# Output projection begun between the score groups of the last head pair

## The chip, the cores and the metric

The kernel runs on one core of one Trainium2 chip. The metric is device time in microseconds of one execution. The runs shown of the kernel before lie between 1240.41 and 1241.53 us, with a median of 1241.26 us.

## The reference

Two layers, each a hybrid mixer and a gated feed-forward block, with a layer norm behind each. x is 512 tokens by 1024, all in float32.

```python
proj = x @ w_in
qa = apply_rope(split_heads(qa, 8), cos_a, sin_a)      # 8 heads of 64, ka alike
ya = merge_heads(head_norm(dilated_attention(qa, ka, va)))
yr = merge_heads(head_norm(retention(qr, kr, vr))) * silu(gr)
yg = merge_heads(head_norm(og)) * silu(rg)             # og: gated linear attention
y = concatenate([ya, yr, yg], -1) * mix_scale          # 512 + 256 + 256 columns
mix = y @ w_out
x = layer_norm(ALPHA * x + mix, ln1_g, ln1_b)
ffn = (silu(gate) * val) @ w_down                      # gate, val = conv(x @ w_up)
x = layer_norm(ALPHA * x + ffn, ln2_g, ln2_b)
```

The dilated attention's three branches are one softmax over all earlier tokens, with a mask and a multiplicity per distance.

## The kernel before, in words

**Products.** Tokens are cut into 4 tiles of 128, and each product of matrices is three matmuls (`mm3`, L212 to L216): both sides are split into a rounded high part and a low part, and high by high, high by low and low by high are summed in PSUM. A weight tile of 128 x 1024 numbers is loaded by SyncE into one of two `raw` buffers; ScalarE (ACT) casts it to the high part `whi` (L198), and VectorE (DVE) subtracts this to get the low part `wlo` (L199), in five buffers each. So a cast waits until the last matmul that reads a buffer has ended, and a load until the subtraction that reads its `raw` buffer has. `made` lists the last matmul of every `mm3`.

**The attention.** The 8 heads of `ya` are handled in 4 pairs. For a pair, `scores` (L626 to L668) makes the scores of the 4 query tiles in three groups: tile 3, tile 2, and tiles 0 and 1 together, for both heads. Each group takes a PSUM bank per head, of four `sm` banks. A group is full matmuls (128 rows) and then matmuls on 64 rows for the low parts. VectorE reads a bank with a mask and takes the maximum (L660), ScalarE takes the exponential (L663), VectorE multiplies by the multiplicity and sums (L664). `weighted` (L669 to L704) transposes the probabilities (L288), ScalarE copies them out (L693), and they are multiplied with the values (L681), in the groups of key tiles (2, 3), (1,) and (0,); then the result is copied (L700) and transposed back. `finish` normalizes it, and `finish_rows` (L711) transposes it to rows `yt[p2]` for the output projection; it is called between the next pair's `scores` and `weighted`, and for pair 3 within `out0`.

**The mixer's end.** While the scores are made, the projections of the other parts run: `v` and the heads of pairs 2 and 3 beside pairs 0 and 1, `gates` beside pair 2. After pair 3's code, four blocks of the gated retention and linear attention, `ynat`, are transposed in the one `side` bank and scaled to rows by `to_rows` (L350 on ScalarE, L351 on VectorE), as `yt[4]` to `yt[7]`. Then `token_gemm` (L394) multiplies the rows with `w_out`, in two halves of 512 columns, `out0` and `out1`: four PSUM banks, one for each token tile, over 8 blocks of rows; for the last `tail` blocks it goes token tile by token tile. `out0` has a tail of 4, `out1` one of 8. `residual` (L390) adds the result to x.

**The order.** A scheduler sets each engine's order when the program is built. Among the instructions it takes for ready it picks that with the lowest priority number, which `at` sets and which counts up with each instruction; what is ready it estimates itself. On the chip each engine runs its order as it stands, and waits on semaphores where data or a buffer is not there. `tc.issue_after(ins)` puts an instruction behind another one of the same engine in that order, without a semaphore. The third score group of pairs 0, 1 and 2 stands behind the 4th, 11th and 4th product of `v`, `heads` and `gates`; that of pair 3 behind nothing.

## Time and profile before

| | before |
|---|---|
| profiled execution | 1243.3 us |
| its span, first to last instruction | 1241.5 us |
| mean granted TensorE clock | 0.995 |
| TensorE matmul busy | 1224.1 us |
| VectorE busy | 794.6 us |
| ScalarE busy | 509.8 us |
| median of three runs | 1241.26 us |

PE is TensorE's matmuls, PEld its weight loads, DVE VectorE, ACT ScalarE, SP SyncE. In an order of time a row has the start in us from the span's start, the duration, engine, source line, operation and tiles; "x3" are merged instructions, and in brackets stands the idle time before, with what ended it. Matmuls overlap, so the distance of their starts tells what one costs, not its duration. In a row of stretches stand the start and end, the length, the busy time of each engine with its number of instructions, and then the granted clock, the DMA share and the GB/s. In a row of waits stand the total, the number and the longest.

### The profile page before, as it was taken

The numbers are of one execution on the slowest core, as the hardware profiler recorded it, in microseconds if no ns is written. First come the engines' busy times: TensorE is split into PE (matmuls) and PEld (weight loads), VectorE is DVE, ScalarE is ACT, GpSimd is POOL, SyncE is SP. The second block draws the span as 40 slices with busy tenths as digits, with TensorE's granted clock in tenths as the row PEclk, the third lists the DMA queues.
The fourth block names the chain that finished last, engine by engine and source line by source line (L and its number), as shares of the span: only waits on it lengthen the run. The fifth ranks groups of instructions, "written<-read, shape, count | busy, mean of one in ns | idle before, by whom it ended". The sixth has DMA issues, their size and how long they took to land.

```text
span 1241.5 us, 15145 instructions
## 1 busy us (share of the span) xinstructions
PE 1224.1 (99%) x5892; PEld 996.8 (80%) x5892; DVE 794.6 (64%) x1467; ACT 509.8 (41%) x721; POOL 17.1 (1%) x26
## 2 busy tenths in 40 slices
PE   9999999999999999999999999999999999999997
PEld 7877777898888888888887777778988888888885
DVE  6697776777663356664767867768766633566636
ACT  4435775144442134442143557652444421444410
POOL 0000000000000000000000000000000000000000
PEclk9999999999999999999999999999999999999998
DMA  8421223223332232322142122231343323333321
GB/s 289 133 66 34 86 86 102 68 85 119 102 91 88 93 115 89 88 99 77 62 128 93 35 58 79 68 119 51 103 120 91 95 77 100 112 102 102 94 77 68
DMA packets 33398, 116.26 MB, mean 94 GB/s; under 512 B 3728, under 2 KB 4144, under 8 KB 33200
## 3 DMA queue, kind: packets, MB, share of 16 engines
q1 hardware_dynamic: 32176, 111.11, 28.5%
q0 software_dynamic: 1152, 4.19, 1.1%
q8 instruction: 46, 0.75, 0.3%
q14 instruction: 24, 0.20, 0.0%
HBM read 113.20 MB, written 2.10 MB: 93 GB/s over the span
## 4 chain that ended last, share of the span: by engine, by line
PE 94%; DVE 3%; ACT 1%; DMA 1%; issue 1%; SPq 0%; DVEq 0%; ACTq 0%
PE acc L214 26%; PE acc L215 26%; PE acc L216 26%; PE bk L288 3%; PE side L214 2%; PE side L216 2%; PE side L215 2%; PE bk L681 2%; PE bk L639 1%; DMA raw<-in_wpk 1%; PE bk L567 1%; PE bk L547 1%; PE bk L563 1%; DVE wlo L199 1%; PE bk L553 1%
## 5 line engine op out<-in xcount | busy, mean ns | idle before, releaser
L199 DVE TENSOR_TENSOR wlo<-raw,whi 128x1024 fp32r<-128x1024 f32 (+2 forms) x201 | 239.9, 1195 | 231.2 <-ACT whi L198 230.5
L215 PE MATMUL acc<-xtl,whi 128*128 128x512 f32 (+1 forms) x896 | 341.9, 382 | 0.0
L214 PE MATMUL acc<-xth,whi 128*128 128x512 f32 (+1 forms) x896 | 340.8, 381 | 0.0
L216 PE MATMUL acc<-xth,wlo 128*128 128x512 f32 (+1 forms) x896 | 340.1, 380 | 0.0
L198 ACT CAST whi<-raw 128x1024 fp32r<-128x1024 f32 (+2 forms) x201 | 205.8, 1026 | 315.8 <-PE side L216 130.7
L216 PEld LDWEIGHTS acc<-xth,wlo 128*128 128x128 f32 x896 | 168.6, 188 | 35.8 <-issue 5.5
L215 PEld LDWEIGHTS acc<-xtl,whi 128*128 128x128 f32 x896 | 168.6, 188 | 33.5 <-issue 3.0
L214 PEld LDWEIGHTS acc<-xth,whi 128*128 128x128 f32 x896 | 168.3, 188 | 32.7 <-issue 2.0
L214 PE MATMUL acc<-whi,xth 128*128 128x512 f32 (+1 forms) x256 | 95.0, 371 | 0.8 <-ACT whi L198 0.8
L215 PE MATMUL acc<-wlo,xth 128*128 128x512 f32 (+1 forms) x256 | 94.9, 371 | 0.8 <-DVE wlo L199 0.7
L216 PE MATMUL acc<-whi,xtl 128*128 128x512 f32 (+1 forms) x256 | 94.1, 368 | 0.0
L214 PE MATMUL acc<-whi,yt 128*128 128x512 f32 x238 | 93.2, 393 | 0.0
L216 PE MATMUL acc<-whi,yt 128*128 128x512 f32 x238 | 92.4, 389 | 0.0
L215 PE MATMUL acc<-wlo,yt 128*128 128x512 f32 x238 | 92.3, 389 | 0.0
L796 DVE SCALAR_TENSOR_TENSOR pg<-acc,prm,pg 128x511 f32<-128x511 f32 x86 | 64.2, 747 | 31.4 <-ACT pg L795 31.4
L795 ACT ACTIVATE pg<-acc,prm 128x512 f32<-128x512 f32 x86 | 66.8, 777 | 26.0 <-PE acc L216 26.0
L797 DVE SCALAR_TENSOR_TENSOR pg<-acc,prm,pg 128x510 f32<-128x510 f32 x86 | 64.4, 749 | 3.0
L390 DVE SCALAR_TENSOR_TENSOR x<-x,acc 128x512 f32<-128x512 f32 x38 | 26.1, 686 | 59.7 <-PE acc L216 59.7
L214 PEld LDWEIGHTS acc<-whi,xth 128*128 128x128 f32 x256 | 48.1, 188 | 9.6 <-issue 1.2
L214 PE MATMUL acc<-whi,yrg 128*128 128x512 f32 x138 | 55.5, 402 | 0.0
L215 PEld LDWEIGHTS acc<-wlo,xth 128*128 128x128 f32 x256 | 48.5, 189 | 8.2 <-DVE wlo L199 1.5
L215 PE MATMUL acc<-wlo,yrg 128*128 128x512 f32 x138 | 54.9, 397 | 0.0
(182 smaller groups left out, 1538.4 us busy)
## 6 DMA issues: line engine op xcount, KB each, us to landing
raw<-in_wpk SPq DMA_DIRECT2D x188, 512.0 KB, 3.6
gb<-in_lnv POOLq DMA_DIRECT2D x8, 512.0 KB, 4.7
x<-in_x SPq DMA_DIRECT2D x4, 512.0 KB, 6.6
raw<-in_wpk SPq DMA_DIRECT2D x8, 256.0 KB, 2.8
out<-x SPq DMA_DIRECT2D x8, 256.0 KB, 2.0
raw<-in_wpk SPq DMA_DIRECT2D x4, 408.0 KB, 3.8
xraw<-in_xt SPq DMA_DIRECT2D x3, 512.0 KB, 7.6
cst<-in_cst SPq DMA_DIRECT2D x1, 1478.0 KB, 9.1
```

Source lines behind the costliest of these rows:

```text
L198: nc.scalar.copy(hi, raw)
L199: lo_engine.tensor_sub(lo, raw, hi.bitcast(F32))
L214: nc.tensor.matmul(ps, ah, bh, start=first, stop=False)
L215: nc.tensor.matmul(ps, ah, bl, start=False, stop=False)
L216: made.append(nc.tensor.matmul(ps, al, bh, start=False, stop=last).ins)
L288: nc.tensor.transpose(dst, src, ident)
L390: V.scalar_tensor_tensor(out=xr, in0=xr, scalar=scale, in1=ps, op0=ALU.mult, op1=ALU.add)
L547: mmul(sc, kT[:, ts], qbd, start=True, stop=True)
L681: mmul(oT[hh * 64:hh * 64 + 64, j * P:], vv[:, j, c0 + hh * 64:c0 + hh * 64 + 64], pts[hh][:, o:o + n], start=j == 2, stop=j == 0, skip_gr ...
L795: A.activation(out=u, in_=ps, func=AF.Identity, scale=w(2), bias=w(3))
L796: V.scalar_tensor_tensor(out=u[:, 1:], in0=ps[:, :S - 1], scalar=w(1), in1=u[:, 1:], op0=ALU.mult, op1=ALU.add)
L797: V.scalar_tensor_tensor(out=u[:, 2:], in0=ps[:, :S - 2], scalar=w(0), in1=u[:, 2:], op0=ALU.mult, op1=ALU.add)
```

## The change

The output projection's first half is made in two parts. Before pair 3's scores the gated blocks are transposed (`turn_gated`) and `out0` is begun: `token_gemm` is now a generator, which stops at the blocks in `pause`. It emits two blocks ahead of the pair's code and the rest behind it. The blocks are taken in the order pair 0, pair 1, gated, pair 2, pair 3, where the gated ones came first, and the weight tiles are packed in that order; `out0` has a tail of 3. The third score group of pair 3 stands behind the 6th product of `out0`. The probabilities' first four batches of transposes of pairs 0 and 2 stand behind the 12th, 14th, 16th and 18th product of `v` and `gates`.

```diff
-        w[f"out{h}"] = [(ks, c) for ks in (PAIRS[2], PAIRS[3], PAIRS[0], PAIRS[1])]
+        w[f"out{h}"] = [(ks, c) for ks in (PAIRS[0], PAIRS[2], PAIRS[3], PAIRS[1])]
...
-    def token_gemm(rows, kt, tail, done, between=None):
+    def token_gemm(rows, kt, tail, done, between=None, pause=()):
...
         for i in range(n - tail):
+            if i in pause:
+                yield
             for t in range(NT):
                 step(i, t)
...
             done(ps[t], t)
+        yield
...
-        def weighted(pr, c0):
+        def weighted(pr, c0, behind):
...
-                    for j in js:
-                        for i in range(j, NT):
-                            transpose(bk[:, o:o + P], pr[hh][i][:, j * P:(j + 1) * P])
-                            o += P
+                    with tc.issue_after(behind.pop(0)) if behind else nullcontext():
+                        for j in js:
+                            for i in range(j, NT):
+                                transpose(bk[:, o:o + P], pr[hh][i][:, j * P:(j + 1) * P])
+                                o += P
...
+        def turn_gated():
+
+            for k in range(4):
+                bk = side()
+                for t in range(NT):
+                    transpose(bk[:, t * P:(t + 1) * P], ynat[t][:, k * P:(k + 1) * P])
+                yt[4 + k] = to_rows(bk, mix(4 + k), "yt" if k == 3 else "yrg")
+
+        order = (0, 1, 4, 5, 6, 7, 2, 3)
...
+        def out_half(h, tail, between=None, pause=()):
...
+            return token_gemm(lambda i: yt[order[i]], kt, tail, done, between, pause)
...
+                p2 = 2 * two + u
+                if p2 == 3:
+                    at(base + 9300)
+                    turn_gated()
+                    at(base + 20000)
+                    marks["out"] = len(made)
+                    out0 = out_half(0, 3, finish_rows, (2,))
+                    next(out0)
                 at(base + 6000 + 3000 * two + 400 * u)
-                p2 = 2 * two + u
...
-                name, n = (("v", 3), ("heads", 10), ("gates", 3), (None, 0))[p2]
-                pr = scores(parts[p2], l3, made[marks[name] + n] if name else None)
+                name, n, m = (("v", 3, 11), ("heads", 10, None), ("gates", 3, 11), ("out", 5, None))[p2]
+                after = lambda n: made[marks[name] + n]
+                pr = scores(parts[p2], l3, after(n))
                 finish_rows()
-                o = weighted(pr, p2 * P)
+                o = weighted(pr, p2 * P, [after(m + 2 * i) for i in range(4)] if m else [])
...
-        order = (4, 5, 6, 7, 0, 1, 2, 3)
...
-            token_gemm(lambda i: yt[order[i]], kt, 8 if h else 4, done, None if h else finish_rows)
+        next(out0)
+        at(base + 25000)
+        next(out_half(1, 8))
```

TensorE, where the first pair's transposes begin, before; `acc` is the product of the second token tile with the values' weights, `pg` the probabilities, `cst` the identity:

```order
L214 MATMUL acc_974<-whi_924,xth_80 128x512
L215 MATMUL acc_974<-wlo_925,xth_80 128x512
L216 MATMUL acc_974<-whi_924,xtl_81 128x512
L288 MATMUL bk_1297<-cst,pg_1250 128x128
L288 MATMUL bk_1297<-cst,pg_1246 128x128 x2
L214 MATMUL acc_974<-whi_930,xth_80 128x512
L215 MATMUL acc_974<-wlo_931,xth_80 128x512
L288 MATMUL bk_1303<-cst,pg_1251 128x128
```

The same place of TensorE's order now:

```order
L214 MATMUL acc_978<-whi_934,xth_80 128x512
L215 MATMUL acc_978<-wlo_935,xth_80 128x512
L216 MATMUL acc_978<-whi_934,xtl_81 128x512
L288 MATMUL bk_1301<-cst,pg_1254 128x128
L288 MATMUL bk_1301<-cst,pg_1250 128x128 x2
L214 MATMUL acc_978<-whi_940,xth_80 128x512
L215 MATMUL acc_978<-wlo_941,xth_80 128x512
```

The first batch stood behind the tile's first 6 matmuls (two blocks of rows), and stands behind 12 now; each further batch follows after six more, where it was two to five. The third pair's batches moved in the same way against the second token tile of `gates`.

TensorE, at the last pair's third score group, before; `bk346` and `bk347` are the third group's banks of the two heads, `acc403` the first token tile of `out0`:

```order
L639 MATMUL bk342_1778<-yrg198_1151,qk197_1150 128x384
L639 MATMUL bk343_1779<-yrg198_1151,qk197_1150 128x384
L639 MATMUL bk346_1802<-qk197_1150 128x256 x2
L639 MATMUL bk346_1802<-yrg198_1151,qk197_1150 128x256 x2
L288 MATMUL side372_1905<-cst_79,yt130_718 128x128
L639 MATMUL bk347_1803<-qk197_1150 128x256 x2
L639 MATMUL bk347_1803<-yrg198_1151,qk197_1150 128x256 x2
L214 MATMUL acc403_1974<-whi392_1952,yrg373_1910 128x512
```

The same place now, where `bk374` is the second group's, `bk378` the third group's bank, and `acc364` and `acc365` belong to `out0`; scores are L643 here:

```order
L214 MATMUL acc364_1836<-whi356_1820,yrg341_1781 128x512
L215 MATMUL acc364_1836<-wlo357_1821,yrg341_1781 128x512
L288 MATMUL side343_1785<-cst_79,yt93_591 128x128
L288 MATMUL side343_1785<-cst_79,yt106_635 128x128
L288 MATMUL side343_1785<-cst_79,yt119_679 128x128
L288 MATMUL side343_1785<-cst_79,yt130_718 128x128
L216 MATMUL acc364_1836<-whi356_1820,yrg342_1782 128x512
L214 MATMUL acc365_1837<-whi353_1814,yt319_1702 128x512
L215 MATMUL acc365_1837<-wlo354_1815,yt319_1702 128x512
L216 MATMUL acc365_1837<-whi353_1814,yt320_1703 128x512
L643 MATMUL bk378_1894<-qk201_1154 128x256
```

The third group followed the second at once. Now 18 matmuls of `out0` and 5 transposes of gated blocks stand between the two. Behind the third group, up to the last batch of transposes of its probabilities that a product waits for first, stand 17 transposes and 15 matmuls, and the fourth token tile of `out0` (in `side`) comes as the last of all, with 21 matmuls in a row.

ScalarE, where the weights of `out1` are cast (`raw410` to `raw419`; the first of them has been cast earlier), before:

```order
L700 COPY pg366_1882<-bk353_1835 128x512
L198 CAST whi414_2099<-raw413_2097 128x1024
L334 ACTIVATE pg368_1890<-bk367_1884 128x512
L198 CAST whi417_2105<-raw416_2103 128x1024
L350 ACTIVATE yt408_2040<-bk407_2035,prm0_86 128x512
L198 CAST whi420_2111<-raw419_2109 128x1024
L198 CAST whi451_2325<-raw450_2323 128x1024
```

And now:

```order
L706 COPY pg398_1974<-bk385_1927 128x512
L334 ACTIVATE pg400_1982<-bk399_1976 128x512
L350 ACTIVATE yt408_2049<-bk407_2044,prm0_86 128x512
L198 CAST whi414_2099<-raw413_2097 128x1024
L198 CAST whi417_2105<-raw416_2103 128x1024
L198 CAST whi420_2111<-raw419_2109 128x1024
L198 CAST whi451_2325<-raw450_2323 128x1024
```

The casts of the second and third tile moved behind the last pair's norm and rows, since the buffers they take are read by the fourth token tile of `out0`. SyncE's loads stand in the same order in both.

## The prediction

> **What bounds the kernel now.** I read the totals first, then the chain of work that ended last, then who waits for whom on TensorE, then the order of time where it waits.

> ```profile
> span 1241.5 us, 15145 instructions
> PE 1224.1 (99%) x5892; PEld 996.8 (80%) x5892; DVE 794.6 (64%) x1467; ACT 509.8 (41%) x721; POOL 17.1 (1%) x26
> PE 94%; DVE 3%; ACT 1%; DMA 1%; issue 1%; SPq 0%; DVEq 0%; ACTq 0%
> PE bk L288 <- DVE s_at L660: 2.3, 4, 0.7
> PE bk L288 <- DVE s_at L664: 1.6, 2, 0.8
> PE bk L639 <- DVE s_at L660: 1.2, 2, 0.6
> ```

> TensorE (PE) is busy for 99% and carries 94% of the chain. VectorE (DVE), at 64%, sets the end only where TensorE stands and waits for it. The change adds or drops no arithmetic: it can only take away waits of TensorE, make new ones, or change the clock. The three rows of waits are the attention's, counted over both layers; 5.1 us in all. The number of waits is twice that of one layer and TensorE's order is the same in both, so I work out one layer and double it.

> **The first pair's transposes.**

> ```profile
> 109.88 0.39 PE L215 MATMUL acc<-wlo,xth 128*128 128x512 f32 x1
> 110.11 0.39 PE L216 MATMUL acc<-whi,xtl 128*128 128x512 f32 x1
> 111.29 0.55 PE L288 MATMUL bk<-cst,pg 128*128 128x128 f32 x3 [0.80 <-DVE s_at L664]
> 111.16 0.08 DVE L664 DVE_READ_ACCUMULATOR2_ANT s_at<- 128x1 f32 x1
> 114.46 0.08 DVE L664 DVE_READ_ACCUMULATOR2_ANT s_at<- 128x1 f32 x1
> ```

> Starts of matmuls lie 0.23 us apart in a stream (109.88 to 110.11). Here the next start comes 1.18 us later, so **0.95 us** is lost, to a softmax step that ends at 111.16 + 0.08 = 111.24. The change puts six more matmuls ahead: 111.29 - 0.95 + 6 x 0.23 = 111.72, after the data. The three later batches follow six matmuls each, the last at about 111.72 + 3 x 1.7 = 116.8, with its data there at 114.54. No semaphore is added, only a place in TensorE's own order. Behind these transposes wait ScalarE's copies, and behind them the products of probabilities and values, whose place is unchanged: 26 matmuls, 6 us, still stand between.

> **The third pair's transposes.**

> ```profile
> 173.82 0.39 PE L216 MATMUL acc<-whi,xtl 128*128 128x512 f32 x1
> 174.85 0.55 PE L288 MATMUL bk<-cst,pg 128*128 128x128 f32 x3 [0.65 <-DVE s_at L660]
> 174.72 0.08 DVE L660 DVE_READ_ACCUMULATOR2_ANT s_at<- 128x1 f32 x1
> 176.52 0.47 PE L215 MATMUL acc<-wlo,xth 128*128 128x512 f32 x1
> 176.90 0.55 PE L288 MATMUL bk<-cst,pg 128*128 128x128 f32 x3
> ```

> The first batch loses 1.03 - 0.23 = 0.80 us, the third 0.38 - 0.23 = 0.15: **0.95**. Six more matmuls put the first at 173.82 + 7 x 0.23 = 175.43, past 174.80, when the bank it needs is free. The batches now end later, but the copy of the last one is needed only behind other products and eight transposes (over 1 us by the row at 179.66 below), which covers it. What else the row with 2.3 holds, waits of the second pair's result, is not touched.

> **The last pair's scores.** The next rows show two places: the first pair, whose third group stands behind products already, and the last pair, where the groups follow each other.

> ```profile
> 100.75 0.96 PE L639 MATMUL bk<-qk 128*128 128x512 f32 x4
> 102.25 0.50 PE L214 MATMUL acc<-whi,xth 128*128 128x512 f32 x1
> 105.14 0.63 PE L639 MATMUL bk<-qk 128*128 128x256 f32 x4
> 106.14 0.50 PE L214 MATMUL acc<-whi,xth 128*128 128x512 f32 x1
> ...
> 196.44 0.96 PE L639 MATMUL bk<-qk 128*128 128x512 f32 x4
> 197.33 0.68 PE L639 MATMUL bk<-yrg,qk 64*128 64x512 f32 x4
> 198.62 0.51 PE L639 MATMUL bk<-qk 128*128 128x256 f32 x2 [0.61 <-DVE s_at L660]
> 199.48 0.33 PE L288 MATMUL side<-cst,yt 128*128 128x128 f32 x1
> 200.69 0.79 PE L214 MATMUL acc<-whi,yrg 128*128 128x512 f32 x1
> ```

> In the first pair the first eight scores take 1.50 us (100.75 to 102.25) and the third group 1.00. In the last pair the same eight hold 2.18, so 0.68 is lost, and the third group takes 2.07 with one transpose of about 0.11 in it, so 0.96 is lost. Then comes what costs most:

> ```profile
> 108.48:111.89 3.41, 2.61 (x13) 1.90 (x13) 3.10 (x13) 3.00 (x6) 0.00 (x0) 1.00 0.00 0
> 197.22:200.63 3.41, 2.78 (x15) 1.62 (x13) 3.27 (x9) 2.47 (x5) 0.00 (x0) 1.00 0.60 179
> 200.63:204.05 3.42, 3.42 (x12) 2.77 (x11) 2.25 (x7) 1.84 (x3) 1.05 (x2) 0.50 0.47 105
> 815.03:818.45 3.42, 3.42 (x14) 2.73 (x13) 2.56 (x9) 2.44 (x4) 0.98 (x2) 0.50 0.63 155
> 179.20:182.60 3.40, 3.40 (x25) 1.80 (x22) 1.44 (x2) 1.55 (x3) 0.00 (x0) 1.00 0.38 111
> ```

> (The number after the POOL column is the granted clock.) Right behind a stretch in which TensorE is busy 2.78 of 3.41 us, partly with half the array's rows (the 64x scores), the clock is 0.50 for 3.42 us, in both layers: 1.71 us lost. Together 0.68 + 0.96 + 1.71 = 3.35 us.

> In the new order 18 matmuls of the output projection, 4.1 us, and five transposes stand between the second and the third group; their first inputs are the first pairs' rows, done long before. The two banks that the third group needs come free within those 4.1 us. So both waits go, and the stretch is full of work with all rows. I give back 0.4 for one score that now runs alone behind four transposes (0.1), and for two to three more changes between kinds of matmul (0.1 to 0.15 each: in the row at 179.66 below, eight transposes take 1.03 where a transpose in the middle takes about 0.11): **2.9 us**, with ends 0 and 3.35.

> **What is late next.** The third group now comes some 4 us later, and VectorE's softmax of it too, while the last transposes wait for that.

> ```profile
> 206.00 0.28 DVE L660 CUSTOM_DVE_ANT_0 pg<-bk,cst 128x128 f32<-128x128 f32 x1
> 206.90 0.75 DVE L351 SCALAR_TENSOR_TENSOR yrg<-side,prm,yrg 128x512 fp32r<-128x512 f32 x1 [0.26 <-ACT yrg L350]
> 207.56 0.28 DVE L664 CUSTOM_DVE_ANT_0 pg<-pg,cst 128x128 f32<-128x128 f32 x1
> 210.68 1.22 DVE L199 TENSOR_TENSOR wlo<-raw,whi 128x1024 fp32r<-128x1024 f32 x1
> 179.66 1.09 PE L288 MATMUL bk<-cst,pg 128*128 128x128 f32 x8
> 180.69 1.92 PE L681 MATMUL bk<-pg,v 128*64 128x384 f32 x8
> ```

> Behind the third group VectorE has, in order: for each head a pair of L660 (0.6: from 206.00 to 206.90, less 0.26 idle) and a pair of L664 (as much, by the equal 0.28 of its first), two L351 (0.66 each, 206.90 to 207.56) and one weight subtraction (1.2): 4.9 us. TensorE has 17 transposes (eight take 1.03, so 2.2) and 15 matmuls (3.4): 5.6 us. The cover is 0.7 us; I cost this at nothing. ScalarE's exponentials can eat that, so it is a rival.

> **The second half's weights.** Its products start at 232.32; call that T. ScalarE's cast of its second tile takes the buffer of the first half's first tile. Before, the last matmul that reads it starts at 215.78; the cast follows at once, with a subtraction of 1.22 (as at 210.68) behind it:

> ```profile
> 215.78 0.40 PE L216 MATMUL side<-whi,yrg 128*128 128x512 f32 x1
> 216.22 1.05 ACT L198 CAST whi<-raw 128x1024 fp32r<-128x1024 f32 x1 [0.31 <-PE side L216]
> 232.32 0.39 PE L214 MATMUL acc<-whi,yrg 128*128 128x512 f32 x1
> raw<-in_wpk SPq DMA_DIRECT2D x188, 512.0 KB, 3.6
> ```

> Now the fourth token tile comes last as a whole, and that reader stands 19 matmuls ahead of T, starting 19 x 0.23 = 4.4 us before T and ending at T - 4.0. Queued behind the waiting cast are the casts of tiles 3, 4 and the next stage's first; the subtraction after it also frees the raw buffer into which SyncE loads tile 4. Cast and subtraction 2.3, load 3.6, cast and subtraction 2.3: T + 4.2. The first product with tile 4's low part stands 19 matmuls behind T: T + 4.4. Five handoffs of about 0.05 (215.78 + 0.40 to 216.22) use that up, so I take a wait of 0.1 us, with ends 0 and 0.7 (a load 0.6 slower).

> **The sum.** Per layer 0.95 + 0.95 + 2.9 - 0.1 = 4.7 us; both layers **9.4**. The profiled execution took 1243.3 us, its span and 1.8 around it; it would take 1233.9. It lies 2.0 above the median of the runs shown, 1241.26, against which I predict: **1231.9 us**.

> **The rivals.**

> *The half clock stays* (or comes at another place): only the waits go, 3.4 us fewer gained, 1235.3. For it: all causes of the drop are inferred, and the new stretch of scores and transposes has few full matmuls. Against it: the first pair's wait of 0.80 (108.48 to 111.89, TensorE busy 2.61) drew no drop, where the rest was full matmuls, and 179.20 to 182.60, with eight transposes and products on half the columns but no wait, was granted 1.00. [...] 14%.

> *VectorE's chain sets the last transposes.* If three exponentials of 0.6 are exposed, 1.8 - 0.7 = 1.1 us a layer: 1234.1; with the weights' 0.7 as well, 1235.3. 10%.

> *The transposes don't gain what they should*, because another bank or copy is late behind them: 3.8 us fewer, 1235.7. 5%.

> *Several of these together*: 3.4 + 2.2 + 1.2 = 6.8 fewer, 1238.7, or a little more. 8%.

> *Slower: the second half's tiles load one after the other.* If the subtraction of its first tile, too, ran only at the end of the first half, tiles 3 and 4 would load in series: 2.3 + 3.6 + 2.3 + 3.6 + 2.3 = 14.1 from T - 4.0, a wait of 5.7 a layer, and after so long a wait a half clock again, 1.7: 14.8 lost against 9.4 gained, 1247. It decides from the point where that subtraction ends after about T - 3.2. Against it: in VectorE's order it stands ahead of the last pair's norm, some 15 us before T. 6%.

> **How the numbers follow.** The forecast has 57%. It and the next three reach from 1229.8 (3.35 regained whole, and nothing new) to 1237.5 (two rivals at once); what is left out is 2 in 10. This kernel's measurement can tell about 0.2%, 2.5 us, from no change, so all below 1238.8 is faster: 57 + 14 + 10 + 5 = 86%; within 8%; slower 6%.

> **What would show it.** On the page of the changed kernel: no wait of the transposes for the softmax's second step, one wait per layer left of the row with 2.3; no wait of a score for VectorE; granted clock 1.00 throughout the last pair. Wrong steps would show as a 0.50 stretch, as a wait of TensorE for a weight cast or subtraction some 4 us into the second half, or as transposes late in the last pair that wait for VectorE or ScalarE.

## The result, and the profile after

The changed kernel takes 1234.61 us, median of 6 runs (1233.9 to 1235.0); the kernel before, on the same chip, 1240.84 us (1239.7 to 1241.6). The ratio is 0.9946, with a 95% interval of 0.9936 to 0.9956: **faster by 0.54%, 6.2 us**. The forecast was 1231.9 us, 2.7 us too low, within its range. The profiled execution after takes 1234.49 us; that of before took 1243.3, so between the two profiles lie 8.8 us, close to the 9.4 forecast, while the medians lie only 6.2 apart, two thirds of it. That the profiles differ by 2.6 us more than the medians is the first thing to explain.

The totals, the engines' shares of the chain and TensorE's waits of the changed kernel (in a row of waits: total, number, longest):

```profile
span 1232.7 us, 15151 instructions
PE 1219.4 (99%) x5892; PEld 994.5 (81%) x5892; DVE 794.5 (64%) x1467; ACT 510.4 (41%) x721; POOL 17.0 (1%) x26
PE 94%; DVE 4%; DMA 1%; issue 0%; ACT 0%; SPq 0%; DVEq 0%; ACTq 0%
...
PE bk L288 <- DVE s_at L664: 1.0, 2, 0.5
...
PE acc L215 <- DVE xtl L386: 0.2, 1, 0.2
```

L664 of the changed kernel is the step that was L660: one wait a layer is left of the row with 2.3, that of the second pair's result. No score waits any more. The last row is new: the up-projection waits for the low part of the normalized tokens.

The places of the prediction in the order of time, first and third pair's transposes, then the last pair's scores:

```profile
111.14 0.39 PE L216 MATMUL acc<-whi,xtl 128*128 128x512 f32 x1
111.38 0.49 PE L288 MATMUL bk<-cst,pg 128*128 128x128 f32 x3
...
175.58 0.39 PE L216 MATMUL acc<-whi,xtl 128*128 128x512 f32 x1
175.81 0.49 PE L288 MATMUL bk<-cst,pg 128*128 128x128 f32 x3
...
193.84 0.96 PE L643 MATMUL bk<-qk 128*128 128x512 f32 x4
194.73 0.68 PE L643 MATMUL bk<-yrg,qk 64*128 64x512 f32 x4
195.34 0.50 PE L214 MATMUL acc<-whi,yt 128*128 128x512 f32 x1
...
200.24 0.62 PE L643 MATMUL bk<-qk 128*128 128x256 f32 x4
200.79 0.50 PE L643 MATMUL bk<-yrg,qk 64*128 64x256 f32 x3
201.22 0.66 PE L288 MATMUL side<-cst,yt 128*128 128x128 f32 x4
```

The transposes follow 0.24 us behind a product, the distance of a stream, where 1.18 and 1.03 stood. The third score group comes at 200.24 with no idle time. The stretches behind the last pair's first scores, where the clock had fallen, are full, at a granted clock of 1.00 (the number after the POOL column):

```profile
196.60:200.01 3.41, 3.41 (x19) 2.82 (x19) 3.41 (x11) 3.14 (x5) 0.00 (x0) 1.00 0.14 53
200.01:203.42 3.41, 3.41 (x25) 2.72 (x24) 3.06 (x13) 2.69 (x7) 0.68 (x2) 1.00 0.00 0
```

In this trace the clock is 1.00 from 6.17 to 1228.14 us and half from there to the end; the last matmul starts at 1223.22, so this half clock costs no product anything. A mean clock of 0.998 is therefore that of an execution without a half clock among its products.

Worked out from the starts in the order of time, the length of each stage in us, layer 1 and layer 2 (the middle column is the profile of the unchanged kernel, run again for the first experiment):

| from, to | before | before again | changed |
|---|---|---|---|
| pair 0's first score, pair 1's | 34.04, 34.10 | 33.90, 34.05 | 32.99, 32.89 |
| pair 2's first score, pair 3's | 32.97, 32.95 | 32.98, 32.95 | 31.69, 31.79 |
| pair 3's first score, first up-product | 59.43, 59.47 | 59.45, 57.95 | 57.06, 57.16 |
| first up-product, next layer's pair 0, or the last matmul | 458.51, 362.46 | 458.52, 362.48 | 458.89, 362.93 |

The third row tells most: of the four stages of the unchanged kernel three take 59.45, and one takes 57.95. That is the stage without a half clock, as the rows of the first experiment show below. So a half clock costs 1.5 us of this stage, where the prediction took 1.71; why it is less is not shown.

### The profile page after: what moved, and what is told of

Same layout as the page of the kernel before. It is cut to its first block, busy times and chain, and to the rows that moved or that the text cites. A ratio compares the mean times of both kernels' runs of the same rounds, so it can differ in the third digit from the quotient of the medians.

```text
span 1232.7 us, 15151 instructions
## 1 busy us (share of the span) xinstructions
PE 1219.4 (99%) x5892; PEld 994.5 (81%) x5892; DVE 794.5 (64%) x1467; ACT 510.4 (41%) x721; POOL 17.0 (1%) x26
## 4 chain that ended last, share of the span: by engine, by line
PE 94%; DVE 4%; DMA 1%; issue 0%; ACT 0%; SPq 0%; DVEq 0%; ACTq 0%
PE acc L214 26%; PE acc L215 26%; PE acc L216 26%; PE bk L288 3%; PE side L216 2%; PE side L215 2%; PE side L214 2%; PE bk L686 2%; PE bk L643 2%; DMA raw<-in_wpk 1%; DVE wlo L199 1%; DVE x L365 1%; PE bk L571 1%; PE bk L551 1%; PE bk L567 1%; PE bk L557 1%
## 5 line engine op out<-in xcount | busy, mean ns | idle before, releaser
L199 DVE TENSOR_TENSOR wlo<-raw,whi 128x1024 fp32r<-128x1024 f32 (+2 forms) x201 | 240.1, 1195 | 225.6 <-ACT whi L198 224.9
L215 PE MATMUL acc<-xtl,whi 128*128 128x512 f32 (+1 forms) x896 | 342.1, 382 | 0.3 <-DVE xtl L386 0.2
L214 PE MATMUL acc<-xth,whi 128*128 128x512 f32 (+1 forms) x896 | 340.8, 381 | 0.0
L216 PE MATMUL acc<-xth,wlo 128*128 128x512 f32 (+1 forms) x896 | 340.1, 380 | 0.0
L198 ACT CAST whi<-raw 128x1024 fp32r<-128x1024 f32 (+2 forms) x201 | 206.0, 1026 | 309.0 <-PE side L216 117.2
L216 PEld LDWEIGHTS acc<-xth,wlo 128*128 128x128 f32 x896 | 168.6, 188 | 35.9 <-issue 5.5
L215 PEld LDWEIGHTS acc<-xtl,whi 128*128 128x128 f32 x896 | 168.6, 188 | 34.3 <-issue 3.0
L214 PEld LDWEIGHTS acc<-xth,whi 128*128 128x128 f32 x896 | 168.3, 188 | 32.7 <-issue 1.9
L214 PE MATMUL acc<-whi,xth 128*128 128x512 f32 (+1 forms) x256 | 96.1, 375 | 0.7 <-ACT whi L198 0.7
L215 PE MATMUL acc<-wlo,xth 128*128 128x512 f32 (+1 forms) x256 | 94.4, 369 | 0.7 <-DVE wlo L199 0.7
L216 PE MATMUL acc<-whi,xtl 128*128 128x512 f32 (+1 forms) x256 | 93.8, 366 | 0.0
L214 PE MATMUL acc<-whi,yt 128*128 128x512 f32 x238 | 93.3, 393 | 0.0
L215 PE MATMUL acc<-wlo,yt 128*128 128x512 f32 x238 | 93.1, 391 | 0.0
L216 PE MATMUL acc<-whi,yt 128*128 128x512 f32 x238 | 92.6, 390 | 0.0
L214 PEld LDWEIGHTS acc<-whi,xth 128*128 128x128 f32 x256 | 48.1, 188 | 10.9 <-issue 2.9
L214 PE MATMUL acc<-whi,yrg 128*128 128x512 f32 x138 | 54.8, 397 | 0.0
L215 PEld LDWEIGHTS acc<-wlo,xth 128*128 128x128 f32 x256 | 48.2, 188 | 8.1 <-DVE wlo L199 1.1
L216 PEld LDWEIGHTS acc<-whi,xtl 128*128 128x128 f32 x256 | 48.1, 188 | 7.6
## 6 DMA issues: line engine op xcount, KB each, us to landing
raw<-in_wpk SPq DMA_DIRECT2D x188, 512.0 KB, 3.6
gb<-in_lnv POOLq DMA_DIRECT2D x8, 512.0 KB, 4.7
x<-in_x SPq DMA_DIRECT2D x4, 512.0 KB, 6.4
xraw<-in_xt SPq DMA_DIRECT2D x3, 512.0 KB, 7.3
```

The source lines that it names most:

```text
L198: nc.scalar.copy(hi, raw)
L199: lo_engine.tensor_sub(lo, raw, hi.bitcast(F32))
L214: nc.tensor.matmul(ps, ah, bh, start=first, stop=False)
L215: nc.tensor.matmul(ps, ah, bl, start=False, stop=False)
L216: made.append(nc.tensor.matmul(ps, al, bh, start=False, stop=last).ins)
```

## The experiments

Two theories stood against each other. A: the two half-clock stretches of the first profile are not in every run, so their 3.4 us were credited too high, and the waits are priced about right. B: the half clock is in every run, and the waits are worth less than priced.

**The kernel before, unchanged.**

> The kernel before, unchanged; it is run to see the granted clock and the span of each of its runs. Theory A (the half clock comes and goes): the two half-clock stretches of 1.7 us each that the profiled execution showed are drawn in some runs only, so the runs fall into groups some 1.7 us apart, near 1240 us with a mean clock of 0.998, near 1241.5 with 0.997, near 1243 with 0.995. Rival B (the half clock is in every run, and the waits were priced too high): every run shows 0.995, and the scatter of 2 us has nothing to do with the clock. Either way the median is 1240 to 1242 us.

Its median was 1240.24 us over 11 runs. Over all experiments 52 runs of the kernel before have a time and a clock:

| mean clock | runs | us |
|---|---|---|
| 0.998 | 26 | 1239.42 to 1240.50, median 1239.9 |
| 0.996, 0.997 | 19 | 1241.12 to 1242.15, median 1241.6 |
| 0.994, 0.995 | 7 | 1242.84 to 1243.65, median 1243.0 |

Three groups, 1.7 and 1.4 us apart, each at its own clock: A holds, and B falls. The new profile shows one execution with both cases; it took 1241.26 us, in the middle group. The rows of stretches of the last pair, layer 1 and then layer 2:

```profile
196.92:200.33 3.41, 2.78 (x14) 1.67 (x15) 3.31 (x9) 2.70 (x4) 0.00 (x0) 1.00 0.49 161
200.33:203.75 3.42, 3.42 (x11) 2.73 (x12) 2.06 (x8) 1.98 (x4) 1.04 (x2) 0.50 0.48 133
811.31:814.73 3.42, 2.97 (x13) 2.07 (x14) 3.08 (x9) 3.20 (x5) 0.30 (x1) 1.00 0.33 132
814.73:818.14 3.41, 3.41 (x25) 2.90 (x24) 3.35 (x14) 3.24 (x6) 0.74 (x2) 1.00 0.64 213
```

11 matmuls in a stretch at half clock, 25 in the same place at full clock. If the groups are runs with none, one and two half-clock stretches, their mean number per run is (19 + 2 x 7) / 52 = 0.63. A stretch is worth 1.55 us, half the distance of the outer groups, so the mean is worth 0.63 x 1.55 = 1.0 us, not 3.4. The first profile, at 0.995 and 1243.3 us, belongs to the third group.

**The transposes alone.** Of the kernel before:

```diff
-                o = weighted(pr, p2 * P)
+                m = (11, None, 11, None)[p2]
+                o = weighted(pr, p2 * P, [made[marks[name] + m + 2 * i] for i in range(4)] if m else [])
```

(The lines of the change in `weighted` belong to this edit too.)

> Only the transposes of the first and third pair are put behind given products; the output projection and the last pair stay as before. Theory A: the waits of 0.95 us for each of these pairs and layer go, 3.8 us (4.7 by how far the places lie apart in the two traces): 1236.2 to 1237.0 us against 1240.8, ratio 0.9962 to 0.9970. The clock still varies from run to run, 0.995 to 0.998, since the last pair's scores still wait. Rival B: the waits were priced too high and only 1.5 to 2.5 us go: 1238.3 to 1239.3 us.

Median 1237.49 us (1237.36 to 1238.9), ratio 0.9974 [0.9963, 0.9984]. In runs without a half clock that is 2.4 us below 1239.9: less than A said, and what B said; the median lies between the two forecasts. The trace shows a wait that neither theory had. TensorE, then VectorE:

```profile
178.35 0.40 PE L216 MATMUL acc<-whi,xtl 128*128 128x512 f32 x1
179.42 0.33 PE L288 MATMUL side<-cst,yt 128*128 128x128 f32 x1 [0.67 <-DVE yt L747]
...
177.54 1.22 DVE L199 TENSOR_TENSOR wlo<-raw,whi 128x1024 fp32r<-128x1024 f32 x1
178.68 0.69 DVE L747 TENSOR_TENSOR yt<-yt,rope 128x512 f32<-128x512 f32 x1
```

With the probabilities moved back, the scheduler brought the first transpose of the gated blocks forward, from 182.54 in the first profile to 179.42. The row of the first profile:

```profile
182.54 0.33 PE L288 MATMUL side<-cst,yt 128*128 128x128 f32 x1
```

Its data come from the gates, which VectorE finishes at 178.68 + 0.69, behind a weight subtraction. The start comes 1.07 us after the product where a stream has 0.23: 0.84 us a layer, 1.7 in all. So this was no clean test of the transposes: the edit had moved a fifth row.

**The transposes alone, the gated ones later.** Of the kernel just shown:

```diff
-        at(base + 9200)
+        at(base + 9300)
         for k in range(4):
             bk = side()
```

> As the kernel with the transposes alone, but the transposes of the gated blocks rank behind the gates in the scheduler's order, as they do in the changed kernel; the last pair's scores and the output projection stay as before. In the kernel with the transposes alone the first of them had been moved 3.1 us ahead, where TensorE waited 0.84 us for it in each layer. Theory A: this wait is what took 1.7 us of the gain. Without it the transposes give 4.1 us, 1235.8 us in runs without a half clock (1239.9 for the kernel before in such runs), and since the last pair still waits, some runs draw one or two half clocks and lie near 1237.5 or 1239.2 with a mean clock of 0.996 or 0.994. Rival: the time is taken somewhere else, VectorE being late as a whole, and 1237.4 us stays the fastest group.

Median 1235.76 us (1235.21 to 1237.38, 5 runs), beside 1240.46 us for the kernel before; ratio 0.9960 [0.9946, 0.9975]. Three runs at a clock of 0.997 lie at 1235.21 to 1235.76; the other two, at 0.996, are 1.0 to 2.2 us above. The stages of pairs 0 and 2 take 33.02, 33.16 and 31.72, 31.81 us, as in the changed kernel. So **the transposes give about 4.3 us** against 1239.9, and as much by the stages, against the first profile; the wait for the gates had taken the rest, and with the last pair's waits in place the half clock still comes, in layer 1 of this profile:

```profile
194.41:197.82 3.41, 2.78 (x14) 1.67 (x15) 3.31 (x9) 2.66 (x4) 0.00 (x0) 1.00 0.55 159
197.82:201.23 3.41, 3.41 (x11) 2.73 (x12) 2.04 (x7) 1.94 (x4) 1.04 (x2) 0.50 0.52 123
805.39:808.80 3.41, 2.78 (x15) 1.61 (x13) 2.74 (x7) 2.40 (x4) 0.00 (x0) 1.00 0.66 243
808.80:812.22 3.42, 3.42 (x21) 2.76 (x20) 3.22 (x10) 3.15 (x6) 1.05 (x2) 1.00 0.15 61
```

**The output projection alone.** Of the changed kernel:

```diff
-                name, n, m = (("v", 3, 11), ("heads", 10, None), ("gates", 3, 11), ("out", 5, None))[p2]
+                name, n, m = (("v", 3, None), ("heads", 10, None), ("gates", 3, None), ("out", 5, None))[p2]
```

> Only the output projection's part: begun ahead of the last pair's scores, third score group behind its 6th product, changed order of blocks, tail of 3. The transposes of the first and third pair are placed freely as before. Theory A: the waits of the last pair give 1.3 us over both layers, and the half clock, which the median run of before draws less than once, 0.8 to 1.7 more: 1237.8 to 1238.8 us against 1240.8, and the clock is 0.998 in every run. Rival B: all of the 3.4 us of half clock are gained too: 1236 us or less.

Median 1238.95 us (1237.82 to 1239.73, 11 runs), ratio 0.9978 [0.9969, 0.9987]: just above A's range, far from B's. No run shows a clock under 0.997, and the profiled one has no half-clock stretch before its last 7.1 us, which begin behind its last product and give it its 0.997. Against 1239.9 only 0.9 us are left of the waits. Its stages say why. From pair 3's first score to the first up-product it takes 57.11 and 56.97 us; against the 57.95 of a stage without a half clock that is 0.84 and 0.98 gained, 1.8 us in all. But from the first up-product on it takes 459.07 and 362.83, 0.9 us more than the kernel before. The place:

```profile
253.06 0.28 PE L214 MATMUL acc<-xth,whi 128*128 128x256 f32 x1
253.66 0.39 PE L215 MATMUL acc<-xtl,whi 128*128 128x256 f32 x1 [0.32 <-DVE xtl L386]
```

The second start comes 0.60 us after the first, where the kernel before has 0.11:

```profile
255.87 0.28 PE L214 MATMUL acc<-xth,whi 128*128 128x256 f32 x1
255.98 0.28 PE L215 MATMUL acc<-xtl,whi 128*128 128x256 f32 x1
```

Half of the wait's gain is given back 50 us later, to the normalization's low part: the first of these products comes 2.81 us earlier than in the kernel before, but VectorE begins the low part only 1.68 us earlier (252.92 against 254.60).

**The third group tied to no product.** Of the changed kernel:

```diff
-                name, n, m = (("v", 3, 11), ("heads", 10, None), ("gates", 3, 11), ("out", 5, None))[p2]
+                name, n, m = (("v", 3, 11), ("heads", 10, None), ("gates", 3, 11), ("out", None, None))[p2]
...
-                pr = scores(parts[p2], l3, after(n))
+                pr = scores(parts[p2], l3, after(n) if n else None)
```

> The changed kernel, but the last pair's third score group is tied to no product: the scheduler puts one head's part behind the 1st and the other's behind the 2nd product of the output projection instead of both behind the 6th. Theory A: what matters is that products that are ready stand there at all. In the changed kernel VectorE frees the two banks 0.6 and 1.8 us after the second group's end, and with one score group and two products between, TensorE just meets them: 1234.6 us as the changed kernel, within 0.6, no wait of a score over 0.2 us, clock 0.998. Rival: the place behind the 6th product is what does it. Then 0.7 to 1.0 us of waits a layer come back, 1236 to 1236.5 us, and with the half clock in some runs up to 1239.

Median 1236.12 us (1235.73 to 1236.33), ratio 0.9958 [0.9944, 0.9971]; 1.5 us above the changed kernel's 1234.61, the rival's number by another way. No score waits, as A said, but products start late 5 us further on, for ScalarE (ACT):

```profile
202.66 0.69 ACT L350 ACTIVATE yrg<-side,prm 128x512 fp32r<-128x512 f32 x1 [0.80 <-PE side L288]
...
203.02 0.40 PE L216 MATMUL acc<-whi,yrg 128*128 128x512 f32 x1
203.40 0.51 PE L214 MATMUL acc<-whi,yrg 128*128 128x512 f32 x1
...
205.45 0.48 PE L215 MATMUL acc<-wlo,yt 128*128 128x512 f32 x1
205.91 0.50 PE L214 MATMUL acc<-whi,yt 128*128 128x512 f32 x1
```

The products that stood behind the third group wait for the scaled gated rows, 0.38 - 0.23 = 0.15 and 0.46 - 0.23 = 0.23 us a layer. The last pair's stage takes 57.70 and 57.60 us, 0.54 more a layer than in the changed kernel; so 1.1 of the 1.5 us lie there, and 0.4 are elsewhere. The tie to the 6th product matters, for what comes after it rather than for the scores.

**Two steps further, and the changed kernel beside them.** First the second pair's result behind a product, then in addition an earlier turn to columns:

```diff
-                finish_rows()
+                finish_rows(after(5) if p2 == 2 else None)
...
-                if t >= 2 and i == n - tail + 3:
+                if t >= 2 and i == n - tail + (3 if t == 2 else 2):
```

> The changed kernel unchanged, beside the two others on the same chip. Theory A: no run draws a half clock, so its runs lie within 1.2 us of each other, 1234 to 1235.2 us, with a mean clock of 0.997 or 0.998 in each, while the kernel before beside it falls into groups near 1240, 1241.5 and 1243 again. Rival: the changed kernel draws a half clock too, only more rarely: single runs near 1236.3 with 0.996.

> The changed kernel, with one wait more taken away: the transposes of the second pair's result, which stand right behind the third pair's last scores and wait 0.5 us for a bank in each layer, are put behind the 6th product of the gates. Theory A (a wait of TensorE that goes is gained whole, as long as the next data are there): 0.5 us a layer, 1.0 us in all, 1233.6 us against 1234.6 for the changed kernel, and no wait of these transposes is left in its trace. Rival: the rows of scaled results are made later on ScalarE and VectorE, these push the softmax of the third pair back, and its transposes wait again: 1234.6 us or more.

> As the kernel with the second pair's result behind the 6th product of the gates, and in addition the normalized third token tile is turned to columns one product (three matmuls, 0.7 us) earlier in each half that ends a block, so that its low part is subtracted ahead of the next stage's weight. Theory A: the changed kernel's new wait of the up-projection's first low product (0.27 and 0.34 us, with 0.1 around each) goes: 0.6 to 0.8 us below the kernel without this edit, about 1232.9 us. Rival: the transposes now wait for the normalization instead, and nothing is gained: 1233.6 us or more.

(The token tile that is turned earlier is the second, not the third.) The three ran on one chip, beside a kernel before of 1241.42 us:

| kernel | median us, 5 runs | ratio to before |
|---|---|---|
| changed kernel | 1234.81 (1234.16 to 1237.51) | 0.9953 [0.9939, 0.9966] |
| with the result behind | 1234.36 (1234.27 to 1234.99) | 0.9947 [0.9934, 0.9959] |
| with the columns earlier too | 1233.74 (1233.25 to 1234.20) | 0.9941 [0.9927, 0.9954] |

Of the changed kernel one run of these five took 1237.51 us at a clock of 0.996, where the rival had 1236.3: a lower clock, drawn rarely, in 1 of its 11 runs. It lies 2.9 us above the median of the other four, more than one half clock's 1.5. What it lost, and where, is not known, since that run has no trace.

That the changed kernel's other runs show no half clock could be luck of the place at which a stretch of 3.41 us begins, and two traces bear on that. In the kernel before, the half clock followed stretches that began 0.79 to 1.52 us after the last pair's first score (the last section has all of them). In the changed kernel run again, layer 1, a stretch begins 1.03 us after this score, and with the result behind, layer 2, one begins 0.85 us after it. Both are full, and so is what follows, at a clock of 1.00:

```profile
194.89:198.30 3.41, 3.41 (x17) 2.42 (x18) 3.41 (x9) 2.88 (x5) 0.00 (x0) 1.00 0.48 159
198.30:201.72 3.42, 3.42 (x23) 2.74 (x21) 3.23 (x11) 2.65 (x5) 0.00 (x0) 1.00 0.00 0
803.75:807.16 3.41, 3.41 (x17) 2.42 (x17) 3.08 (x7) 2.29 (x4) 0.00 (x0) 1.00 0.61 183
807.16:810.57 3.41, 3.41 (x21) 2.54 (x20) 3.41 (x13) 3.21 (x5) 0.00 (x0) 1.00 0.00 0
```

The result behind a product gains 0.25 to 0.45 us, not 1.0: the wait of 0.5 goes, the stage of pair 2 shortens by 0.3 a layer (31.44, 31.45), and the low product of the up-projection is again late:

```profile
250.57 0.28 PE L214 MATMUL acc<-xth,whi 128*128 128x256 f32 x1
251.13 0.39 PE L215 MATMUL acc<-xtl,whi 128*128 128x256 f32 x1 [0.29 <-DVE xtl L386]
```

The third kernel takes this wait away. Its low part stands ahead of the weight subtraction on VectorE, and the products run on:

```profile
249.21 0.68 DVE L386 TENSOR_TENSOR xtl<-bk,xth 128x512 fp32r<-128x512 f32 x1
249.81 0.15 DVE L318 SCALAR_TENSOR_TENSOR s_ln<-s_ln,s_ln 128x1 f32<-128x1 f32 x1
249.88 0.68 DVE L386 TENSOR_TENSOR xtl<-bk,xth 128x512 fp32r<-128x512 f32 x1
250.48 0.15 DVE L319 SCALAR_TENSOR_TENSOR s_ln<-s_ln,s_ln 128x1 f32<-128x1 f32 x1
250.54 1.22 DVE L199 TENSOR_TENSOR wlo<-raw,whi 128x1024 fp32r<-128x1024 f32 x1
...
250.76 0.28 PE L214 MATMUL acc<-xth,whi 128*128 128x256 f32 x1
250.88 0.28 PE L215 MATMUL acc<-xtl,whi 128*128 128x256 f32 x1
```

Its median is 0.6 us below the second's, as A said for this edit, and 1.1 us below the changed kernel's. The absolute 1232.9 was missed because the second kernel's 1.0 had not come. The intervals of the three ratios overlap, so a ranking rests on the traces more than on the times; still, all five runs of the third kernel lie below every run of the second.

## Why the prediction was near, and what was off

*What bounds the kernel, and where it waits:* right. Each wait named is gone from the rows of waits.

*The first and third pair's transposes, 0.95 a layer each, 3.8 in all:* right in mechanism, a little small. The stages are 1.05 and 1.21, and 1.28 and 1.16 us shorter than in the first profile, 4.7; the experiment with the transposes alone shows 4.3 in the time. What the prediction did not see: the gated blocks' transposes had to stay behind the gates for it. The change ranks them later, and without that 1.7 us are lost.

*The last pair's scores, 2.9 a layer:* the waits went as said. Of the 0.68 + 0.96 - 0.4 = 1.24 without the clock, 0.89 and 0.79 came (57.95 to 57.06 and 57.16): the give-back was more than the 0.4 priced (0.06 and 0.19 of it are the weights' waits below).

*The clock's 1.71 a layer:* **the step that failed.** The prediction took the two half-clock stretches of one profiled execution as part of every run, and then took the 2.0 us, by which this execution lay above the median, off the result again, as an offset that would stay. They were the same microseconds: the profiled run had drawn two stretches, the median run of the three, 1241.26, by its time one, and half of the 52 runs none. The size was off as well: by the stages a stretch costs 1.5 us, not 1.71. Counted from the profile, without the offset, the sum gave 1233.9, and the changed kernel takes 1234.6. The offset alone is 2.0 of the 2.7 us of error.

*The second half's weights, a wait of 0.1 with ends 0 and 0.7:* right. In layer 2 the product with the fourth tile's low part comes 0.42 after its neighbour, 0.19 us late; in layer 1 it is 0.06 late:

```profile
840.48 0.39 PE L214 MATMUL acc<-whi,yt 128*128 128x512 f32 x1
840.90 0.50 PE L215 MATMUL acc<-wlo,yt 128*128 128x512 f32 x1
```

*What is late next:* VectorE's chain did not set the last transposes: in the changed kernel they start at 207.51, 0.23 us after the product ahead of them, without a wait. So that rival falls, though its 1234.1 us is nearer to the measured 1234.6 than the forecast. What the prediction left out is the next stage. In the changed kernel TensorE waits for the low part of the second token tile, which VectorE makes behind a weight subtraction:

```profile
249.34 1.22 DVE L199 TENSOR_TENSOR wlo<-raw,whi 128x1024 fp32r<-128x1024 f32 x1
250.54 0.69 DVE L386 TENSOR_TENSOR xtl<-bk,xth 128x512 fp32r<-128x512 f32 x1
...
250.90 0.28 PE L214 MATMUL acc<-xth,whi 128*128 128x256 f32 x1
251.28 0.39 PE L215 MATMUL acc<-xtl,whi 128*128 128x256 f32 x1
```

Here 0.27 us and in layer 2 0.34 are lost, and with them this stage is 0.38 and 0.47 us longer. That the order of VectorE is the cause is shown by the last kernel, where the low part stands ahead of the subtraction and the wait is gone; this stage is 0.35 us shorter in each layer there than in the kernel without that edit.

*The rivals by time alone.* A half clock that stays was put at 1235.3 us, also nearer to 1234.6 than the forecast. The time could not have told the two apart; the clock of the runs and the full stretches do. The low end of the forecast's range, 1229.8, does not follow from its own terms either: 3.35 in place of 2.9 and nothing for the weights is 1.1 us less than 1231.9, so 1230.8.

*The 8.8 us between the profiles* are near the 9.4 in part by luck. The transposes gave 0.9 more than forecast, the stage of the last pair 4.7 instead of 5.6 (the weights' wait counted in), and what stands behind it lost 0.85 where nothing was forecast. Another 0.3 us comes from ahead of the first score (100.75 to 100.42), which the prediction did not have.

The sum, in stages against an execution without a half clock: 2.3 + 2.4 from the transposes, 1.7 from the last pair, less 0.85 behind it, 5.5 us. The times say 1239.9 - 1234.6 = 5.3. The half clock adds 1.0 on average, and 1.7 where the median run is one of the middle group. So about four fifths of what the waits gave (4.3 of 5.3) is the transposes' part, though the output projection is the larger edit; that adds some 1 us of waits, and the 1.0 of half clock.

## What to carry to other kernels

Before a profiled execution's excess over the median is taken as an offset, look for what in that execution could come and go; a stretch at half clock is such a thing (here 1.5 us, and 0.63 of them a run by the three groups), and it must be weighted with its share of the runs. A wait that goes from one stage is gained only as far as the slower engine's next delivery allows (with the projection alone, 0.9 of 1.8 us went to the wait for VectorE's low part), so follow the chain to the next stage, not only to the end of the edit. And when rows of a scheduled order are moved, look at what the scheduler puts into the free place.

## What the runs showed of the hardware

How large each group should be cannot be worked out from this alone. In the first profile the two layers' last pairs lie 613.66 us apart, so layer 2's stretch begins 0.73 us later behind its first score than layer 1's. But layer 1 drew a half clock there; without it, by the 1.5 us of the stage, the shift would be some 2.2 us (an estimate). That the stretch's place is even over the runs is not shown either.

The busy time of TensorE in the stretch does not decide it. The one from 805.39 to 808.80 above, with 2.78 us busy and 15 matmuls, drew nothing; 197.22 to 200.63 of the first profile, also 2.78 and 15, did. The longest idle time in a stretch that drew a half clock is 0.61 us. Which of the two in it is needed, the wait or the scores on half the rows, was not separated: the changed kernel has no such wait, and its third score group stands 4.2 us further back, out of these stretches.
